# Letting background steps in between projection matmuls half as often, in bursts of up to twice the size

## The chip, the cores and the metric

The kernel runs on one core of one Trainium2 chip. The metric is the device time of one execution in microseconds (us), the median of several runs. PE is the matmul engine (TensorE), DVE is VectorE, ACT is ScalarE, POOL is GpSimd, and SP is the engine whose queue issues the transfers from HBM.

## What is computed

Two layers over 256 latent tokens and 256 context tokens of width 1024. Each layer is a token mixer and then an expert-choice mixture of 16 experts (MoE). The second layer needs the context only as keys, so its mixer works on 256 columns where the first works on 512. The reference, cut to the mixer:

```python
dq, dk, dv, hy, sq, sk, sv, gt = split_in(h @ p['w_in'])
q = apply_rope(dq.reshape((B, L) + qk_shape), cos, sin)
y_diff = diff_post(diff_latent(q, concat(k, kc), concat(v, vc), lam), ...)
y_hy = hyena(hy, p)                                   # short conv, long conv by a DFT
y_swa = swa_latent(s_q, s_k, s_v, s_kc, s_vc, sink)   # windowed attention with a sink
gs = jnp.split(sigmoid(gt), 3, axis=-1)
merged = sum(gs[b] * (ys[b] @ p['w_branch'][b]) for b in range(3))
y = merged @ p['w_out']
```

## The kernel before, in words

The program has no loop at run time. Python code writes out one fixed order of instructions for every engine, and a planner in it (`Model`, `Background`) decides that order while the program is being built: it keeps a guessed clock for each engine and guesses when each tile will be ready. On the chip every engine then works through its own list in that order and waits on semaphores where an operand is late.

A mixer is a list of 116 blocks (`mixer`). A block makes 128 output columns of one projection: its weights are loaded by SP (tile `wraw`), split by ACT, DVE and POOL into a high and a low part (`wh`, `wl`), and multiplied on PE in 24 matmuls into one PSUM bank, 8 of `wh` with `hhi`, 8 of `wh` with `hlo`, then 8 of `wl` with `hhi` (`yb` and `mg` take the place of `hhi` and `hlo` in later blocks). Blocks 0 to 52 of the mixer feed the attention and Hyena tasks, the later ones are gates, `w_branch` products, eight blocks for the windowed attention, and last, blocks 108 to 115, `w_out`.

Everything else of the mixer is background: tasks written as Python generators (`diff_gen`, `swa_gen`, `hyena_gen`, `filter`, `mod_run`, `mod_vec`). A task issues one **step** (some instructions on one or more engines) and then yields the tiles that its next step needs. A typical step issues a pair of score matmuls (`kp`, `kl` with `qp`), or the four transposes of a probability tile (a matmul of `cst` with an `arena` tile), or the product with the values (`arena` with `svt`), or only the ACT and DVE work between these.

Steps come into PE's list in four ways:

- `pump` (L367), called between the matmuls of a block and once after it: it takes steps whose tiles the planner thinks ready, while a credit lasts, while ACT and DVE are not too far behind, and at most `BURST` steps that used PE.
- `until` (L383), ahead of a block's matmul whose operand is late: it fills the gap.
- `slot` (L392), when the work behind a block (its evacuation, `b.evac`) needs a buffer of the arena and none is free: it forces the step that can run first, ready or not, until one is free.
- `drain` (L399): block 92 of the second mixer begins the third branch, which needs the windowed attention's results, so all of its remaining steps are forced there in one piece.

The calls between a block's matmuls stand at the end of the loop over `i` from 0 to 15, where `k` is `i % 8`; for `i` below 8 a pass issues two matmuls, from 8 on one:

```python
if i < KT or k % 2 and k < KT - 1:
    self.bg.pump()
```

The MoE's weights (tile `mw`) are first asked for late in the mixer, after certain blocks (`PREF`, L46, and `fill` at L1053): in the first mixer after blocks 108 to 111, in the second after blocks 87, 93, 108, 111 and 112. The rest is asked for as the MoE frees buffers.

Of the kernel before, what the change touches and what calls it, by code (L numbers as in the profile page):

```python
# [21 lines left out]
KT = 8  # L22
# [4 lines left out]
WCUT = (4, 4)  # L27
WIDTH = (4, 3)
BACKLOG = (1500.0, 750.0)
BURST = (6, 3)  # L30
SWA = 8
SWA_STEP = 2
RATE = (0.75, 0.6)
# [253 lines left out]
class Background:  # L287
# [79 lines left out]
    def pump(self, rate=None):  # L367
        self.credit = min(self.credit + (self.now - self.mark) * (rate or self.rate()), CREDIT[self.layer])
        n = 0
        while n < BURST[self.layer]:  # L370
            self.start()
# [37 lines left out]
class Kernel:  # L409
# [588 lines left out]
    def run_blocks(self, bl, ahead=2, first=3):  # L998
        nl = ns = first
        later = []  # L1000
        for j, b in enumerate(bl):
            self.bg.due, end = [], self.bg.now
            for c in bl[j:]:
                if c.drains:
                    self.bg.due.append((c.drains, end))
                end += 24 * (4.0 + 0.41 * c.n)
            while ns < min(max(j + ahead, first + (j > 0)), len(bl)):
                self.split_block(bl[ns], later if j else None)
                ns += 1
            while nl < len(bl) and (nl <= ns or (nl - ns < 3 and self.model.dead("a4", BUFS["a4"]) > SPARE[self.bg.layer])):  # L1010
                self.load_block(bl[nl])
                nl += 1
            if self.bg.layer and len(bl) - 1 - j == MODR:
                self.bg.add("mod", lambda task: self.mod_vec([(1, v) for v in range(3, 6)]))
            if j < first:
                while later:
                    later.pop(0)()
                if j == 0:
                    for c in bl[:first]:
                        if c.pre:  # L1020
                            c.pre()
                    hi, lo = b.hl()
                    ps = [self.bank([128, c.n], "d" if i < 2 else "b") for i, c in enumerate(bl[:first])]
                    for k in range(KT):
                        self.bg.until([hi[:, k], lo[:, k]])
                        for c, p in zip(bl, ps):
                            self.mm3(p, (c.wh[:, k], c.wl[:, k]), (hi[:, k, 0:c.n], lo[:, k, 0:c.n]), k == 0, k == KT - 1)
                b.wh = b.wl = None
                b.evac(ps[j])
                continue  # L1030
            if b.pre:
                b.pre()
            hi, lo = b.hl()[:2]
            p = self.bank([128, b.n], "d")
            for i in range(2 * KT):
                k = i % KT
                if i < KT:
                    self.bg.until([b.wh[:, k], hi[:, k], lo[:, k]])
                    self.mm(p, b.wh[:, k], hi[:, k, 0:b.n], i == 0, False)
                    self.mm(p, b.wh[:, k], lo[:, k, 0:b.n], False, False)  # L1040
                else:
                    self.bg.until([b.wl[:, k]])
                    self.mm(p, b.wl[:, k], hi[:, k, 0:b.n], False, k == KT - 1)
                if i >= LATER[self.bg.layer] and later:
                    later.pop(0)()
                if i > LATER[self.bg.layer] and nl < len(bl) and nl - ns < 3 and self.model.dead("a4", BUFS["a4"]) > SPARE[self.bg.layer]:
                    self.load_block(bl[nl])
                    nl += 1
                if i < KT or k % 2 and k < KT - 1:
                    self.bg.pump()  # L1050
            b.wh = b.wl = None
            if len(bl) - 1 - j in PREF[self.bg.layer]:
                self.fill(PREF[self.bg.layer][len(bl) - 1 - j])  # L1053
            b.evac(p)
            self.bg.pump()
# [1008 lines left out]
```

## Time and profile before

| | |
|---|---|
| median of 3 runs | 2575.46 us (2573.92 to 2581.18) |
| the profiled execution | 2579.04 us |
| its span, first to last instruction | 2577.3 us |
| PE busy | 2240.2 us, 87% of the span |
| DVE, ACT, POOL busy | 52%, 34%, 31% |
| granted PE clock, mean | 0.945 |
| first mixer, first projection matmul to the MoE | about 42 to 985 us |
| first MoE | about 985 to 1507 us |
| second mixer | about 1507 to 2102 us |
| second MoE and the end | about 2102 to 2577 us |

The profile is of one execution, taken by the hardware profiler. An engine's share is an average over four stages that have different limits, so it is read stage by stage. "Idle before" an instruction is the time its engine stood still just ahead of it, put down to what ended that wait. L458 is the helper that issues matmuls, L469 the one that issues transposes, and L261 the one through which all other engines' instructions go, so groups are told apart by their tiles.

### The profile page before, as it was taken

How to read it: one execution, taken by the hardware profiler on the slowest of the kernel's cores; microseconds unless marked ns; L12 is line 12 of the kernel's file. 1: busy time of each engine (PE TensorE's matmuls, PEld its weight loads, DVE VectorE, ACT ScalarE, POOL GpSimd, SP SyncE). 2: the span in 40 equal slices, each digit the busy share in tenths (PEclk: the TensorE clock that was granted, in tenths of full speed). 3: DMA queues.
4: the chain of work that ended last, by engine and by line, in shares of the span. 5: the costliest groups of instructions: out<-in, count | busy, mean ns of one | idle time of the engine just before them, and what ended most of it. 6: DMA issues, size and time to landing. Idle time of an engine off the chain costs nothing.

```text
span 2577.3 us, 38619 instructions
## 1 busy us (share of the span) xinstructions
PE 2240.2 (87%) x14970; PEld 1542.7 (60%) x14970; DVE 1347.2 (52%) x2907; ACT 882.1 (34%) x1933; POOL 794.8 (31%) x775
## 2 busy tenths in 40 slices
PE   6999998989999998989998899899888987656565
PEld 4777776767768775333333378878787864323223
DVE  4778778888672324223333178887887541101011
ACT  4445444555552332101111055556435441000001
POOL 2653433642334541000111055665544430000000
PEclk8999999999999999999999999999989989878787
DMA  9434233221213368899999963333665589999997
GB/s 304 123 122 126 89 109 106 58 66 50 66 58 91 95 252 316 331 428 417 398 400 399 398 185 97 104 95 84 177 190 164 130 317 423 422 424 423 424 423 278
DMA packets 327135, 590.32 MB, mean 229 GB/s; under 512 B 46076, under 2 KB 278184, under 8 KB 299304
## 3 DMA queue, kind: packets, MB, share of 16 engines
q1 hardware_dynamic: 326952, 587.85, 62.2%
q8 instruction: 119, 1.95, 0.3%
q14 instruction: 64, 0.52, 0.1%
HBM read 584.66 MB, written 3.15 MB: 228 GB/s over the span
## 4 chain that ended last, share of the span: by engine, by line
PE 47%; DMA 20%; DVE 20%; issue 4%; ACT 4%; POOL 3%; SPq 1%; DVEq 0%; POOLq 0%; ACTq 0%
PE p L458 44%; DMA mw<-in_moe_w_dram 19%; DVE arena L261 6%; DVE t L261 5%; PE p L469 3%; DVE wl L261 2%; DVE qp L261 2%; ACT arena L261 1%; DMA wm<-in_w_mod_dram 1%; POOL wl L261 1%; SPq L261 1%; POOL arena L261 1%; DVE ma L261 1%; DVE yc L261 1%; ACT wh L261 1%
## 5 line engine op out<-in xcount | busy, mean ns | idle before, releaser
L458 PE MATMUL p<-mw,xg 128*32 128x256 f32 (+1 forms) x3072 | 411.0, 508 | 115.3 <-DMA mw<-in_moe_w_dram 114.4
L458 PE MATMUL p<-hhi,wh 128*128 128x512 f32 (+1 forms) x1344 | 471.4, 363 | 10.1 <-DVE arena L261 7.7
L458 PE MATMUL p<-hlo,wh 128*128 128x512 f32 (+1 forms) x1344 | 458.9, 354 | 1.6 <-POOL hlo L261 0.8
L261 POOL TENSOR_TENSOR wl<-wraw,wh 128x512 fp32r<-128x512 f32 x232 | 342.5, 1478 | 374.8 <-ACT wh L261 251.8
L458 PEld LDWEIGHTS p<-mw,xg 128*32 128x32 f32 (+1 forms) x3072 | 133.7, 129 | 317.1 <-issue 200.0
L458 PE MATMUL p<-hhi,wl 128*128 128x512 f32 (+1 forms) x1344 | 312.9, 361 | 4.5 <-DVE wl L261 4.4
L458 PEld LDWEIGHTS p<-hhi,wh 128*128 128x128 f32 x1344 | 259.4, 193 | 48.5 <-issue 13.3
L458 PEld LDWEIGHTS p<-hlo,wh 128*128 128x128 f32 x1344 | 259.6, 193 | 31.4 <-POOL hlo L261 1.7
L458 PE MATMUL p<-mw,aT 128*32 128x256 f32 (+3 forms) x1760 | 200.4, 475 | 62.5 <-DMA mw<-in_moe_w_dram 58.2
L261 DVE TENSOR_TENSOR wl<-wraw,wh 128x512 fp32r<-128x512 f32 x231 | 217.0, 940 | 57.4 <-ACT wh L261 47.0
L261 ACT ACTIVATE wh<-wraw 128x1024 fp32r<-128x1024 f32 x232 | 241.4, 1053 | 9.0 <-DMA wraw<-in_w_in_dram 6.8
L458 PEld LDWEIGHTS p<-hhi,wl 128*128 128x128 f32 x1344 | 222.0, 194 | 37.0 <-DVE wl L261 5.2
L261 ACT ACTIVATE arena<-p 128x512 f32<-128x512 f32 (+1 forms) x212 | 106.4, 507 | 354.5 <-PE p L458 296.7
L458 PEld LDWEIGHTS p<-mw,aT 128*32 128x32 f32 (+1 forms) x1760 | 79.5, 134 | 172.3 <-issue 109.0
L261 DVE COPY yS<-p 32x512 f32<-32x512 f32 (+1 forms) x60 | 33.4, 556 | 272.9 <-ACT yS L261 272.9
L261 POOL TENSOR_TENSOR sq<-sq,sq 128x512 f32<-128x512 f32 (+1 forms) x6 | 6.3, 1055 | 505.6 <-ACT sq L261 498.8
L458 PE MATMUL p<-yb,wh 128*128 128x512 f32 (+1 forms) x768 | 153.6, 343 | 7.5 <-POOL yb L261 6.8
L261 ACT ACTIVATE arena<-p,t 128x512 f32<-128x512 f32 (+1 forms) x192 | 116.5, 613 | 84.7 <-DVE t L261 82.5
L458 PEld LDWEIGHTS p<-yb,wh 128*128 128x128 f32 x768 | 118.5, 190 | 26.8 <-POOL yb L261 11.6
L261 ACT ACTIVATE s<-p 128x512 f32<-128x512 f32 (+1 forms) x32 | 15.7, 491 | 337.1 <-PE p L458 336.9
L261 ACT ACTIVATE yS<-p 32x256 f32<-32x256 f32 (+2 forms) x84 | 35.3, 420 | 266.2 <-PE p L458 247.1
L469 PE MATMUL p<-cst,arena 128*128 128x128 f32 x608 | 101.0, 290 | 28.8 <-DVE arena L261 27.8
(243 smaller groups left out, 3451.4 us busy)
## 6 DMA issues: line engine op xcount, KB each, us to landing
mw<-in_moe_w_dram SPq DMA_DIRECT2D x171, 2048.0 KB
wraw<-in_w_in_dram SPq DMA_DIRECT2D x152, 512.0 KB
wm<-in_w_mod_dram SPq DMA_DIRECT2D x72, 512.0 KB
mw<-in_moe_w_dram SPq DMA_DIRECT2D x46, 512.0 KB
mw<-in_moe_w_dram SPq DMA_DIRECT2D x17, 1024.0 KB
wraw<-in_w_branch_dram SPq DMA_DIRECT2D x32, 512.0 KB
wm<-in_w_mod_dram SPq DMA_DIRECT2D x5, 2048.0 KB
wraw<-in_w_in_dram SPq DMA_DIRECT2D x32, 256.0 KB
```

The costliest lines, as they stand in the source:

```text
L261: return f(*args, **kw)
L458: self.nc.tensor.matmul(out, lhsT=lhsT, rhs=rhs, start=start, stop=stop, skip_group_check=tiles > 1)
L469: self.nc.tensor.transpose(out, in_, self.ident[:n, :n])
```

## The change

```diff
-BURST = (6, 3)
+BURST = (12, 6)
...
-                if i < KT or k % 2 and k < KT - 1:
+                if k % 2 and i < KT or k == 3 and i > KT:
                     self.bg.pump()
```

The two numbers of `BURST` are for the first and the second layer. Before, `pump` is called behind `i` = 0 to 7 and 9, 11 and 13, which is 11 times in a block; with the change behind `i` = 1, 3, 5, 7 and 11, which is 5 times. The call behind the evacuation of a block stays. The `BURST` bound also holds for the calls inside the MoE.

No instruction is added or taken away; they come in another order. Three places show it, all on PE. In the names, `p` is a PSUM bank, `wh` and `wl` are a block's weights, `hhi` and `hlo` the projection's input, `cst` with `arena` a transpose, `kp` or `kl` with `qp` scores, `arena` with `svt` a product with the values.

The second mixer, inside block 69, before, from the middle of its `wh` matmuls on:

```order
L458 MATMUL p_15403<-hlo_11520,wh_15342 128x256
L469 MATMUL p_15415<-cst_68,arena_11588 128x128 x4
L458 MATMUL p_15403<-hhi_11519,wh_15342 128x256
L458 MATMUL p_15403<-hlo_11520,wh_15342 128x256
L469 MATMUL p_15427<-cst_68,arena_11588 128x128 x4
L458 MATMUL p_15432<-kp_14684,qp_15258 128x512
L458 MATMUL p_15432<-kl_14685,qp_15258 128x512
```

The same block with the change, its last rows and the first of what stands between it and block 70:

```order
L458 MATMUL p_15285<-hlo_11520,wh_15230 128x256
L458 MATMUL p_15285<-hhi_11519,wl_15231 128x256 x8
L469 MATMUL p_15315<-cst_68,arena_11588 128x128 x4
L469 MATMUL p_15327<-cst_68,arena_11589 128x128 x4
L469 MATMUL p_15335<-cst_68,arena_11589 128x128 x4
L458 MATMUL p_15344<-arena_11588 128x128 x4
L458 MATMUL p_15351<-kp_14525,qp_15325 128x512
L458 MATMUL p_15351<-kl_14526,qp_15325 128x512
```

Before, two insertions stand between the matmuls of block 69 and none behind it. With the change the block runs without a break, and behind it stand 34 background matmuls in one piece, which the evacuation's wish for an arena buffer forces out.

The second mixer, between blocks 91 and 92 (the drain), its beginning before:

```order
L458 MATMUL p_16639<-yb_15784,wl_16568 128x256 x8
L458 MATMUL p_16679<-kp_16293,qp_16513 128x512
L458 MATMUL p_16679<-kl_16294,qp_16513 128x512
L458 LDWEIGHTS identb_407
L458 MATMUL p_16679<-mask_406,identb_407 128x128
L458 MATMUL p_16680<-kp_16293,qp_16513 128x512
L458 MATMUL p_16680<-kl_16294,qp_16513 128x512
L458 LDWEIGHTS identb_407
L458 MATMUL p_16680<-mask_406,identb_407 128x128
L469 MATMUL p_16696<-cst_68,arena_11589 128x128 x4
L469 MATMUL p_16702<-cst_68,arena_11589 128x128 x4
L469 MATMUL p_16715<-cst_68,arena_11588 128x128 x4
```

The same place with the change:

```order
L458 MATMUL p_16535<-yb_15704,wl_16491 128x256 x8
L469 MATMUL p_16583<-cst_68,arena_11588 128x128 x4
L469 MATMUL p_16591<-cst_68,arena_11588 128x128 x4
L469 MATMUL p_16603<-cst_68,arena_11588 128x128 x4
L469 MATMUL p_16609<-cst_68,arena_11588 128x128 x4
L458 MATMUL p_16614<-arena_11589,svt_14207 64x128
L458 MATMUL p_16614<-arena_11588,svt_14207 64x128
```

Two more attention tasks are left for the drain: it holds 164 matmuls before and 208 with the change, and from the tile `p_16696` on the two lists hold the same steps.

## Rows read from the trace of the kernel before

**Rows 1.** Busy time by stretch: from:to, us; then busy us of each engine, PEclk, DMA share, GB/s
```profile
62.00:985.00 923.00, 877.57 (x4762) 684.51 (x4762) 615.08 (x1332) 425.64 (x955) 401.44 (x396) 0.99 0.34 104
985.00:1507.00 522.00, 475.03 (x2531) 197.21 (x2533) 170.18 (x421) 78.55 (x179) 47.47 (x73) 0.97 0.96 387
1523.00:1982.00 459.00, 419.17 (x2863) 375.23 (x2863) 386.75 (x700) 236.18 (x458) 265.83 (x227) 0.96 0.46 135
1986.00:2025.00 39.00, 30.09 (x230) 23.08 (x229) 29.98 (x84) 22.31 (x61) 5.00 (x10) 0.82 0.07 21
2025.00:2102.00 77.00, 76.12 (x601) 71.11 (x600) 31.75 (x58) 36.91 (x81) 46.69 (x39) 1.00 0.91 284
2102.00:2577.00 475.00, 301.70 (x3630) 148.02 (x3628) 71.12 (x209) 42.65 (x120) 3.26 (x5) 0.82 0.96 397
```

**Rows 2.** Waits of PE, 62 to 985 us: waited for, us in total, times, longest us
```profile
PE p L469 <- DVE arena L261: 10.2, 12, 3.0
PE p L458 <- DVE qp L261: 6.6, 9, 2.0
```

**Rows 3.** Waits of PE, 1523 to 2102 us
```profile
PE p L469 <- DVE arena L261: 17.6, 16, 2.8
PE p L458 <- DVE arena L261: 8.2, 5, 3.3
PE p L458 <- DVE wl L261: 4.4, 4, 2.9
```

**Rows 4.** Waits of PE, 2102 to 2577 us
```profile
PE p L458 <- DMA mw<-in_moe_w_dram: 149.1, 72, 5.8
```

**Rows 5.** PE in order of time, second mixer, the drain: start us, us, instruction [idle before]
```profile
1986.69 0.23 PE L458 MATMUL p<-mask,identb 128*128 128x128 bf16 x1
1988.08 1.06 PE L469 MATMUL p<-cst,arena 128*128 128x128 f32 x8 [1.17 <-DVE arena L261]
1991.01 1.39 PE L469 MATMUL p<-cst,arena 128*128 128x128 f32 x8 [1.86 <-DVE arena L261]
...
2003.25 1.06 PE L469 MATMUL p<-cst,arena 128*128 128x128 f32 x8 [0.98 <-DVE arena L261]
...
2019.41 3.44 PE L469 MATMUL p<-cst,arena 128*128 128x128 f32 x16 [2.06 <-DVE arena L261]
...
2024.68 0.39 PE L458 MATMUL p<-hhi,wh 128*128 128x256 f32 x1
```

**Rows 6.** PE in order of time: steps let in between matmuls without a wait
```profile
608.31 1.09 PE L458 MATMUL p<-arena,svt 128*64 128x128 f32 x16
609.34 0.66 PE L469 MATMUL p<-cst,arena 128*128 128x128 f32 x4
609.75 0.71 PE L458 MATMUL p<-hhi,wl 128*128 128x512 f32 x2
...
1978.93 0.40 PE L458 MATMUL p<-kp,qp 128*128 128x512 f32 x1
...
1981.22 0.36 PE L458 MATMUL p<-hhi,wh 128*128 128x256 f32 x1
```

**Rows 7.** SP's transfers in order of time, around the drain
```profile
1986.59 2.57 SPq L261 DMA_DIRECT2D wraw<-in_w_branch_dram  x4
2026.95 0.35 SPq L261 DMA_DIRECT2D mw<-in_moe_w_dram  x1
...
2078.71 57.19 SPq L261 DMA_DIRECT2D mw<-in_moe_w_dram  x28
```

**Rows 8.** PE in order of time, first mixer: an insertion, then matmuls without one
```profile
600.36 0.38 PE L469 MATMUL p<-cst,arena 128*128 128x128 f32 x2
600.50 0.48 PE L458 MATMUL p<-hhi,wh 128*128 128x512 f32 x1
600.81 0.39 PE L458 MATMUL p<-hlo,wh 128*128 128x512 f32 x1
...
601.49 0.40 PE L458 MATMUL p<-hlo,wh 128*128 128x512 f32 x1
601.72 0.39 PE L458 MATMUL p<-hhi,wh 128*128 128x512 f32 x1
```

## The prediction, made before the changed kernel ran

> **What bounds the kernel now.** I read busy time by stretch first, then PE's waits in each mixer, then PE and SP in order of time around the drain. In both mixers PE is the bound: it is busy 877.57 of 923.00 us in the first and 419.17 of 459.00 us in the second up to its drain, while DMA runs at a third to a half of its time [rows 1]. What PE does not work there is 45.4 and 39.8 us, in short waits, mostly for DVE: 12 of them last 10.2 us and 16 last 17.6 us, so 0.85 and 1.1 us each [rows 2, 3]. The drain is a stretch of its own: in 39.00 us PE is busy for 30.09, at a granted clock of 0.82, so a part of it at the lower of its two levels, 1.2 GHz, after waits of 1 to 2 us [rows 1, 5]. The second MoE waits 149.1 us for its weights [rows 4], with DMA at 0.96 of its time [rows 1]. Does a longer mixer then cost anything? Yes: through the drain SP issues nothing of `mw` (none between 1986.59 and 2026.95), and 28 of its loads start only at 2078.71 [rows 7], behind blocks that PE reaches only after the drain. The first MoE's weights are asked for behind blocks 108 to 111. So PE time won or lost in either mixer moves all that follows by as much.
>
> **The change, part by part.** The work is the same: between the first and the last projection matmul the order holds 1534 background matmuls in the first mixer and 785 in the second, both before and after, and the same transfers. Only places move. There are 113 blocks behind the first three, so `pump` is called 113 x 12 = 1356 times in a mixer before and 113 x 6 = 678 times with the change. Yet the order shows 259 insertions in the first mixer and 99 in the second before, and 207 and 80 with the change: most calls found nothing to take. So insertions fall by 71, a fifth, not by half.
>
> *Fewer insertions.* Behind a transpose the next projection matmul takes 0.31 us to its successor's start (600.50 to 600.81), in an unbroken run 0.23 (601.49 to 601.72) [rows 8]. 71 x 0.08 = 5.7 us won. Not every kind of step costs that much, so it is 3 to 6; I take 5.5.
>
> *The drain.* Before, from the end of its first score pair at 1986.92 to 2024.68 it takes 37.8 us [rows 5]. It holds 16 groups of transposes, 8 products with the values and 5 more score pairs. Where such steps are let in without a wait, a product takes 1.03 us (608.31 to 609.34), a group of transposes 0.41 (609.34 to 609.75), and two score pairs 2.29 (1978.93 to 1981.22) [rows 6], so this work would take 8 x 1.03 + 16 x 0.41 + 5 x 1.15 = 20.5 us. The drain loses 17.3 us on it, through waits and the lower clock: 0.60 us for each of the 29 groups, 0.11 us for each of 158 matmuls. With the change 44 more matmuls stand there: 44 x 0.11 = 4.8 us. Their 2 tasks could fit into waits that are there anyway (0). Or they make one more whole round like the one from 2003.25 to 2019.41, 16.2 us [rows 5] with some 9 us of work in it (3 products, 3 pairs, 6 transpose groups), a loss of 7. I take 5. What is issued less between the blocks before it is PE time given back, and is left out of both sides.
>
> A rule of the Trainium skill speaks against this change: the page "Perfetto Trace Analysis", section "Optimization Strategy", says that performance may be improved by interleaving stretches with different busiest engines. Taken by the words of the change, half the interleaving would be lost: half of 1534 + 785 matmuls at the drain's 0.11 us would be some 127 us by that reading, an estimate. The drain agrees with the rule's direction; that so much cover is lost is not borne out, since the order leaves all but some 160 of these matmuls between or behind blocks as they were.
>
> *Runs forced by a full arena.* Background that progresses later holds its buffers longer. Behind blocks 39 and 45 of the first mixer and 41 and 69 of the second, where the evacuation asks for a buffer, the new order has runs of 20, 30, 28 and 34 matmuls in one piece between a block's last `wl` matmul and the next block's first. Before, the only such run stands behind block 73 of the second mixer, 20 long, with data mostly there. The new runs have 24 groups in all (a Hyena product, then its transposes, then `mod` or attention steps), that depend on each other through ACT and DVE as in the drain. At the drain's 0.60 us a group that is 14 us. If every group waited as an average wait in the first mixer, 24 x 0.85 = 20 us; if the steps were ready, 0. I take 12, near the drain, as a few of the groups are of tasks that do not wait for each other.
>
> *Steps let in later.* A call now comes every second pair of matmuls, so a step is let in on average half a pair-time later: one matmul of 512 columns, 0.23 us [rows 8], in the first mixer, half of that in the second. A wait of 0.85 us shrinks by at most 0.23, or 27% of 45.4 = 12 us; 0.12 of 1.1 us is 11% of 39.8 = 4 us. So up to 16 us are won. Against it: more steps at once put a longer line into DVE, which ends most waits, and in that line stand the split of the weights (4.4 us of waits) and the evacuation of the blocks (within 8.2 us) [rows 3]. The same 16 us bounds it from above. I take 3 us won.
>
> *The higher bound of a burst* costs nothing by itself: the mean insertion grows only from 5.9 to 7.4 matmuls and from 7.9 to 9.8. In the first mixer SP's loads of `wm` and of the filter stand elsewhere among the `wraw` loads; the cover is a DMA share of 0.34 [rows 1]. If that went, a late `wraw` would show as a wait for `wh`, and PE has none worth a row now.
>
> Sum: 5 + 12 - 5.5 - 3 = 8.5 us. On the profiled execution's own 2579.0 us that is 2587.5. The median shown is 2575.5, 3.6 us below it, so the forecast is 2584 us, 0.33% slower. About 0.3% (8 us) is what a measurement of this kernel can tell from no change, so the forecast lies at that edge.
>
> **The rivals.** *Faster, by waits that vanish.* If the waits in the mixers are mostly steps let in a little too early, the full 16 us come back, and the forced runs cost nothing because what they hold is ready: 5 - 5.5 - 16 = -16.5, 2559 us; with half of the runs' price -10.5, 2565 us. For it: nearly all waits are for DVE and short. Against it: 0.23 us is little beside 0.85. It decides once the forced runs cost under 6 us in all.
>
> *It does little.* Insertions fall by only a fifth. If forced runs cost 6 instead of 12 us the sum is 2.5 us: 2578 us, nothing to be told. For it: before, the first mixer has runs of 24 and 26 matmuls that were let in ready, with no loss of the drain's kind.
>
> *Slower, by a queue on DVE.* The bursts delay evacuations and weight splits. Then the two rows of 8.2 and 4.4 us [rows 3] double, the waits do not shrink, and the forced runs cost 20 us: 5 + 20 - 5.5 + 12.6 = 32 us, 2608 us. For it: three waits of a projection's first matmul for a bank that DVE frees are among the longest of the second mixer (up to 3.3 us). Against it: `pump` still stops while DVE is behind.
>
> **How the numbers follow.** The forecast's own case (forced runs at 8 to 16 us, waits about as before) has 0.42, the queue on DVE 0.10, little effect 0.28, faster 0.20. Its own range is 2578 to 2592. The forecast case reaches a little under the edge and the case of little effect a little over it, which cancel: slower by over 0.3% 0.52, within 0.28, faster 0.20. The ends with all bounds together are 5.5 + 16 = 21.5 us won (2554) and 7 + 20 + 16 - 3 = 40 us lost (2616). Cutting a tenth from each side gives 2562 to 2604.
>
> **What would show it.** Right: PE's drain lasts 47 to 55 us instead of 39 with its clock still near 0.8; behind blocks 39, 45, 41 and 69 stand runs with waits on DVE and ACT of 2 to 4 us in sum each; PE's total work is unchanged; both MoEs last as long as before, moved. Wrong: idle time in the mixers outside these runs falls by over 10 us, or grows by it; PE waits for `wh` or `wraw`; or the second MoE starts later but ends no later.

## The result, and the profile after

The changed kernel takes 2600.48 us (median of 4 runs, 2596.33 to 2603.86); the kernel before, on the same chip, 2577.01 us (2573.92 to 2581.18). The ratio is 1.0088 with a 95% interval of 1.0072 to 1.0104, so the change costs 0.0088 x 2577.0 = 22.7 us, between 18.6 and 26.8. The forecast was 2584 us, 8.5 us more than before: the sign and the main places were right, the size was too small by a factor of 2.7. The measured time lies above the forecast case's own range (2578 to 2592 us), and near the slow end of the whole range (2562 to 2604).

The busy time by stretch of the changed kernel, in the columns of [rows 1]:

```profile
62.00:998.00 936.00, 886.37 (x4767) 690.84 (x4766) 623.54 (x1332) 425.81 (x956) 398.04 (x397) 0.99 0.34 103
998.00:1517.00 519.00, 475.95 (x2527) 197.72 (x2529) 169.29 (x418) 77.62 (x177) 47.52 (x73) 0.97 0.96 389
1534.00:1994.00 460.00, 414.98 (x2814) 371.12 (x2813) 381.29 (x677) 230.37 (x441) 259.17 (x224) 0.96 0.47 134
1997.00:2049.00 52.00, 36.52 (x292) 27.84 (x293) 42.22 (x115) 28.92 (x80) 7.11 (x14) 0.87 0.04 11
...
2125.00:2598.00 473.00, 298.28 (x3632) 144.40 (x3630) 71.19 (x209) 42.68 (x121) 3.52 (x5) 0.82 0.96 398
```

The first mixer is 13 us longer, the drain lasts 52 us instead of 39 with a granted clock of 0.87, and the two MoEs are 3 and 2 us shorter. To compare like with like, two stretches are cut at the same matmuls in every kernel: "first mixer" is the start of the first matmul of block 3 to that of block 108, "second mixer" that of block 3 to that of block 92, the drain included. The kernel before, in the same columns:

```profile
62.00:932.82 870.82, 825.93 (x4517) 645.37 (x4517) 598.13 (x1302) 401.16 (x878) 383.35 (x381) 0.99 0.32 94
1523.18:2024.68 501.50, 452.79 (x3121) 401.80 (x3121) 420.24 (x789) 261.01 (x525) 271.62 (x237) 0.95 0.43 125
1982.74:2024.68 41.94, 33.03 (x255) 25.84 (x253) 32.93 (x90) 25.02 (x68) 5.97 (x10) 0.84 0.09 26
```

The changed kernel:

```profile
62.34:945.46 883.12, 834.02 (x4518) 651.11 (x4517) 606.25 (x1302) 400.99 (x878) 379.74 (x381) 0.98 0.31 93
1534.34:2048.42 514.08, 453.26 (x3120) 400.83 (x3121) 423.09 (x789) 261.82 (x525) 266.29 (x238) 0.95 0.43 122
1993.61:2048.42 54.81, 38.98 (x314) 30.10 (x313) 42.10 (x113) 31.97 (x86) 7.46 (x14) 0.88 0.07 20
```

In each, the third row is block 91 and the drain behind it. The two profiled spans differ by 2597.6 - 2577.3 = 20.3 us, and it adds up: first mixer +12.3, the stretch to the second mixer (945.46 to 1534.34, before 932.82 to 1523.18) -1.5, second mixer up to block 91 -0.3, block 91 with the drain +12.9, all behind it -3.4, the start +0.3. PE's work in numbers of matmuls is the same. In the first mixer PE idles 49.1 us instead of 44.9 and is busy 8.1 us longer; in the second it idles 60.8 instead of 48.7. Ahead of block 91 in the second mixer, PE's busy time falls by 5.5 us and its idle time rises by 5.2.

**The forced runs.** Behind block 45 of the first mixer, PE in order of time, in the columns of [rows 5]:

```profile
451.83 1.18 PE L458 MATMUL p<-hhi,wl 128*128 128x512 f32 x4
452.94 0.64 PE L458 MATMUL p<-wm,sc 128*32 128x256 f32 x8
455.06 0.68 PE L458 MATMUL p<-arena,arena 128*128 128x128 f32 x4 [1.48 <-DVE arena L261]
455.50 1.67 PE L458 MATMUL p<-yf,ft 128*128 128x256 f32 x12
458.24 0.66 PE L469 MATMUL p<-cst,yt 128*128 128x128 f32 x4 [1.07 <-ACT yt L261]
458.82 0.64 PE L458 MATMUL p<-wm,sc 128*32 128x256 f32 x8
463.67 1.11 PE L469 MATMUL p<-cst,yd 128*128 128x128 f32 x4 [4.21 <-DVE yd L261]
464.44 0.78 PE L458 MATMUL p<-hhi,wh 128*128 128x512 f32 x1
```

DVE at the same place:

```profile
457.18 2.37 DVE L261 TENSOR_TENSOR arena<-arena,K 128x512 f32<-128x512 f32 x2
459.48 1.72 DVE L261 TENSOR_SCALAR t<-t 128x4 f32<-128x4 f32 x4
461.16 0.16 DVE L261 TENSOR_TENSOR t<-t 128x4 f32<-128x4 f32 x1
461.36 0.16 DVE L261 TENSOR_TENSOR t<-t,t 128x4 f32<-128x4 f32 x1
...
462.73 0.16 DVE L261 SCALAR_TENSOR_TENSOR t<-t,t 128x4 f32<-128x4 f32 x1
462.93 0.69 DVE L261 TENSOR_TENSOR yd<-yd,t 128x512 f32<-128x512 f32 x1
```

PE stands still three times, 6.76 us in all, and the last time for 4.21 us: just as long as DVE needs for a chain of 13 small instructions (a reciprocal root in `t`, 4 values in each partition) and the scaling of `yd`, 459.48 to 463.62. Ahead of that chain in DVE's list stands 2.37 us of another task's product. The run takes 11.5 us (452.94 to 464.44) for work of 4.2 (2 x 0.64, 0.44, 1.67 and two groups of transposes at 0.41 [rows 6]).

The other three runs, each ending with the next block's first matmul. Behind block 39 of the first mixer, 41 and 69 of the second (the row at 1883.51 is still block 69's own):

```profile
389.87 0.51 PE L458 MATMUL p<-yf,ft 128*128 128x256 f32 x3
391.38 0.38 PE L458 MATMUL p<-yf,ft 128*128 128x256 f32 x1 [0.99 <-ACT yf L261]
392.72 1.22 PE L458 MATMUL p<-yf,ft 128*128 128x256 f32 x8 [0.96 <-POOL yf L261]
395.54 1.06 PE L469 MATMUL p<-cst,yd 128*128 128x128 f32 x4 [1.60 <-DVE yd L261]
...
397.11 0.78 PE L458 MATMUL p<-hhi,wh 128*128 128x512 f32 x1
...
1728.45 0.47 PE L458 MATMUL p<-kp,qp 128*128 128x512 f32 x1 [0.39 <-DVE qp L261]
...
1729.66 0.50 PE L458 MATMUL p<-kp,qp 128*128 128x512 f32 x1 [0.50 <-DVE qp L261]
...
1731.16 0.47 PE L458 MATMUL p<-kp,qp 128*128 128x512 f32 x1 [0.30 <-DVE arena L261]
...
1731.81 1.67 PE L458 MATMUL p<-yf,dfth 128*128 128x256 f32 x12
1734.29 0.66 PE L469 MATMUL p<-cst,yt 128*128 128x128 f32 x4 [0.81 <-ACT yt L261]
1738.76 1.11 PE L469 MATMUL p<-cst,arena 128*128 128x128 f32 x4 [3.81 <-DVE arena L261]
1739.53 0.56 PE L458 MATMUL p<-hhi,wh 128*128 128x256 f32 x1
...
1883.51 1.86 PE L458 MATMUL p<-hhi,wl 128*128 128x256 f32 x8 [1.76 <-DVE wl L261]
1885.17 2.47 PE L469 MATMUL p<-cst,arena 128*128 128x128 f32 x12
...
1891.58 0.39 PE L458 MATMUL p<-hhi,wh 128*128 128x256 f32 x1
```

They take 7.2, 11.5 and 6.4 us. The first holds 12 matmuls and 8 transposes, 1.67 + 0.82 = 2.5 us of work. The second runs from 1728.06 to 1739.53: ahead of the same kind of work stand two forced score steps, 8 matmuls of 512 columns (1.8 us at 0.23 each [rows 8]), with waits of 0.39, 0.50 and 0.30 us, so it has 4.3 us of work and waits of 5.8 us in all. The third has no wait in it. So in place the four lose 4.7 + 7.3 + 7.1 + 0 = 19.1 us. The third is not free either: its 12 transposes take 2.47 us, where three groups would take 1.23 [rows 6], but the wait of 1.76 us that precedes them is one of block 69's own matmuls, so this is not added here. Short windows of PE, three behind the runs, one ahead of the run behind block 45, and one over the run behind block 69:

```profile
397.00:403.00 6.00, 6.00 (x32) 4.35 (x31) 4.75 (x8) 2.00 (x3) 3.92 (x3) 0.83 0.01 1
464.00:470.00 6.00, 6.00 (x23) 4.88 (x21) 4.75 (x8) 2.64 (x4) 3.35 (x3) 0.73 0.01 4
1739.00:1745.00 6.00, 6.00 (x31) 5.91 (x31) 3.98 (x8) 2.51 (x5) 3.18 (x2) 0.60 0.05 15
446.00:452.00 6.00, 5.29 (x34) 4.46 (x33) 4.51 (x10) 2.74 (x10) 4.05 (x3) 1.00 0.39 126
1885.00:1892.00 7.00, 6.87 (x55) 5.44 (x55) 6.84 (x14) 2.42 (x6) 0.00 (x0) 0.84 0.44 126
```

In the first three PE is busy for all of the 6 us, at granted clocks of 0.83, 0.73 and 0.60, so 34, 54 and 80% of the time at the lower level, 1.2 GHz. In the 6 us from 446 us, ahead of the run, the clock was 1.00. By an estimate from these clocks the three windows cost another 6 x (0.17 + 0.27 + 0.40) = 5.0 us. But the kernel before has such stretches too, at other places. Added up over windows of 4 us, PE's busy time times what its clock lacked of 1.00 is 7.6 us in the first mixer before and 10.6 with the change, 21.9 and 19.5 in the second: 3.0 us more and 2.4 us less. So over both mixers the lower clock costs about the same in both kernels.

**The drain**, PE in order of time (from 1996.65, where block 91 ends, to the first matmul of block 92):

```profile
1995.53 1.12 PE L458 MATMUL p<-yb,wl 128*128 128x256 f32 x8
2002.76 3.65 PE L469 MATMUL p<-cst,arena 128*128 128x128 f32 x16 [6.11 <-DVE arena L261]
...
2048.42 0.39 PE L458 MATMUL p<-hhi,wh 128*128 128x256 f32 x1
```

Before, the drain began with score matmuls [rows 5] that needed nothing new; now it begins with transposes, and PE waits 6.11 us for the first of them.

**Other waits of PE** in the changed kernel, for the second mixer (1534 to 2123 us) as in [rows 3]:

```profile
PE p L469 <- DVE arena L261: 19.7, 11, 6.1
PE p L458 <- DVE arena L261: 7.7, 4, 5.2
PE p L458 <- DVE wl L261: 4.9, 4, 1.8
```

Over the whole run:

```profile
PE p L469 <- DVE yd L261: 20.0, 12, 4.9
```

The same row before:

```profile
PE p L469 <- DVE yd L261: 8.1, 6, 4.0
```

It is the row that grew most, by 11.9 us. The forced runs hold 5.8 us of it (1.60 and 4.21), and a wait of 4.91 us stands inside block 38 of the second mixer.

### The profile page after: what moved, and what is told of

The parts are those of the page before. It is cut to its first block, busy times and chain, and to the rows that moved or that the text cites. A ratio compares the mean times of both kernels' runs of the same rounds, so it can differ in the third digit from the quotient of the medians.

```text
span 2597.6 us, 38636 instructions
## 1 busy us (share of the span) xinstructions
PE 2245.8 (86%) x14970; PEld 1545.3 (59%) x14970; DVE 1356.8 (52%) x2907; ACT 882.2 (34%) x1933; POOL 785.3 (30%) x775
## 4 chain that ended last, share of the span: by engine, by line
PE 48%; DMA 20%; DVE 18%; ACT 5%; issue 4%; POOL 3%; SPq 1%; DVEq 0%; POOLq 0%; ACTq 0%
PE p L458 45%; DMA mw<-in_moe_w_dram 18%; DVE t L261 5%; DVE arena L261 5%; PE p L469 3%; DVE wl L261 2%; ACT arena L261 2%; DVE qp L261 1%; DMA wraw<-in_w_in_dram 1%; DMA wm<-in_w_mod_dram 1%; ACT wh L261 1%; POOL wl L261 1%; SPq L261 1%; DVE ma L261 1%; DVE yc L261 1%
## 5 line engine op out<-in xcount | busy, mean ns | idle before, releaser
L261 POOL TENSOR_TENSOR wl<-wraw,wh 128x512 fp32r<-128x512 f32 x232 | 332.6, 1435 | 437.1 <-ACT wh L261 357.4
L458 PE MATMUL p<-hhi,wl 128*128 128x512 f32 (+1 forms) x1344 | 307.1, 360 | 6.6 <-DVE wl L261 4.9
L458 PE MATMUL p<-mw,aT 128*32 128x256 f32 (+3 forms) x1760 | 195.2, 460 | 57.5 <-DMA mw<-in_moe_w_dram 53.8
```

What stands on the lines that cost most here:

```text
L261: return f(*args, **kw)
L458: self.nc.tensor.matmul(out, lhsT=lhsT, rhs=rhs, start=start, stop=stop, skip_group_check=tiles > 1)
```

## The experiments

The theory: halving the calls makes the background late, and it is paid for where a late step is forced, by a full arena (behind a block) or by the drain, whether its data are there or not. Rivals: that fewer calls cost by themselves; that longer bursts hold up DVE; that the steps left to the drain are the whole loss. The following table has all twelve runs. A forced group is a step that used PE and was issued by `slot` or `drain`, counted in the order of each kernel; "arena + drain" are those of the second mixer, and one group of each drain count stands only behind block 115. The lengths are those of the stretches above, from each kernel's own profile.

| kernel | calls in a block | `BURST` | ratio to before, 95% interval | first mixer, us (forced) | second mixer, us (arena + drain) | block 91 and drain, us |
|---|---|---|---|---|---|---|
| before | 11 | 6, 3 | 1 | 870.8 (0) | 501.5 (4 + 31) | 41.9 |
| changed | 5 | 12, 6 | 1.0088 [1.0072, 1.0104] | 883.1 (11) | 514.1 (15 + 39) | 54.8 |
| burst_alone | 11 | 12, 6 | 1.0026 [1.0012, 1.0040] | 871.2 (0) | 507.6 (6 + 16) | 24.0 |
| calls_alone | 5 | 6, 3 | 1.0182 [1.0163, 1.0200] | 883.3 (11) | 532.3 (27 + 40) | 57.7 |
| calls_second_only | 11, 5 | 12, 6 | 1.0044 [1.0028, 1.0059] | 868.8 (0) | 512.9 (15 + 39) | 54.0 |
| half_calls_deeper_second | 5 | 12, 6 | 1.0031 [1.0019, 1.0044] | 883.2 (11) | 494.6 (0 + 4) | 10.7 |
| half_calls_deeper_both | 5 | 12, 6 | 1.0007 [0.9994, 1.0020] | 876.6 (0) | 495.5 (0 + 4) | 10.7 |
| before_deeper_both | 11 | 6, 3 | 1.0023 [1.0006, 1.0039] | 872.3 (0) | 502.3 (5 + 1) | 2.9 |
| seven_calls | 7 | 12, 6 | 1.0065 [1.0043, 1.0087] | 873.1 (0) | 511.7 (30 + 8) | 15.9 |
| fifteen_calls | 15 | 6, 3 | 1.0017 [1.0005, 1.0029] | 878.6 (0) | 496.3 (1 + 12) | 25.1 |
| second_5_calls_free | 11, 5 | 6, 6 | 0.9997 [0.9985, 1.0009] | 871.0 (0) | 494.5 (0 + 4) | 10.7 |
| second_7_calls_free | 11, 7 | 6, 6 | 0.9998 [0.9985, 1.0012] | 871.1 (0) | 502.6 (0 + 3) | 7.9 |
| second_11_calls_free | 11 | 6, 6 | 0.9974 [0.9962, 0.9986] | 870.3 (0) | 492.7 (0 + 5) | 13.2 |
| second_15_calls_free | 11, 15 | 6, 6 | 0.9961 [0.9947, 0.9976] | 870.4 (0) | 496.0 (0 + 4) | 7.5 |

Two numbers of calls are for the first and the second mixer. `BACKLOG` is 1500, 750 (ns, one number for each mixer) unless a diff says otherwise: `pump` takes nothing while the work that is queued on ACT and DVE exceeds it by the planner's clock, so a larger number lets more steps in early. All diffs are against the kernel before; where a diff has only `+` lines, the lines that they replace are left out. The same order repeats well: the changed kernel's first mixer stands in three kernels and took 883.1, 883.3 and 883.2 us; that of before stands in seven and took 868.8 to 871.2. The changed kernel's second mixer stands in two (514.1 and 512.9), that of half_calls_deeper_second in three (494.6, 495.5 and 494.5). What follows the second mixer varies more, 547.6 to 552.6 us in the fourteen profiles, partly in other orders.

### The two parts alone

```diff
-BURST = (6, 3)
+BURST = (12, 6)
```

> Only the bound of a burst is raised (12 and 6), the calls stay 11 in a block. PE's order is the same as before up to the second mixer; there the drain holds 82 matmuls instead of 164, and the arena forces a few groups more. Theory (what costs is steps that are forced, in the drain or for an arena buffer): the drain gets 7 to 10 us shorter than its 39 us, forced groups take some of it back, so 2570 to 2580 us, same as before. Rival (larger bursts put a longer line into DVE, and this is what made the change slower): second mixer longer by 8 to 13 us, 2585 to 2590 us, with more idle outside forced runs.

Measured: 2581.33 us, ratio 1.0026. The first mixer is unchanged. In the second the drain shrinks as 82 of its 164 matmuls are let in earlier, yet the mixer is 6.1 us longer:

```profile
1520.83:2028.40 507.57, 449.71 (x3120) 394.59 (x3120) 427.62 (x789) 262.00 (x524) 267.22 (x237) 0.97 0.42 124
```

PE's idle time is 57.9 us there, 9.2 more than before, though fewer groups are forced. So the number of forced groups is not the whole of it. The median lies 1 us above the theory's range and 4 below the rival's, the mixer's 6.1 us below the rival's 8 to 13: a longer line on DVE is not excluded as the cause of these 6 us.

```diff
-                if i < KT or k % 2 and k < KT - 1:
+                if k % 2 and i < KT or k == 3 and i > KT:
```

> Calls halved, burst bound left at 6 and 3. The first mixer's order is that of the change; in the second the order holds 27 groups forced by the arena and 40 in the drain, 67 against 54 with the change. Theory (about 0.6 us lost for each forced group): 8 us longer than with the change, about 2608 us. Rival (the bound of the burst is what costs, the calls do not): no longer than the kernel before in the second mixer, about 2588 us.

Measured: 2621.52 us, ratio 1.0182, 13 us more than the 2608 expected. The halved calls alone cost some 47 us (0.0182 x 2573.4), twice the whole change:

```profile
1535.83:2068.17 532.34, 463.08 (x3120) 408.14 (x3120) 411.31 (x789) 260.55 (x524) 266.93 (x237) 0.93 0.40 118
```

The first mixer is the changed kernel's; the second is 18.2 us longer still, at a clock of 0.93. So the two parts do not add up (0.26% and 1.82%, together 0.88%): with half the calls the higher bound of a burst gives back some 24 us. The forced groups of the second mixer fall with it from 67 to 54; that the late steps catch up by it is argued from that.

### One mixer at a time

```diff
+BURST = (12, 6)
+                if (k % 2 and i < KT or k == 3 and i > KT) if self.bg.layer else (i < KT or k % 2 and k < KT - 1):
```

> Calls halved in the second mixer alone, burst bound raised in both: the first mixer's order is that of before, the second's that of the change. Theory (each mixer loses by its own forced runs): half of the loss stays, the first mixer is back at about 943 us, the second as long as with the change, 2585 to 2592 us. Rival (the loss comes from one cause shared by both, so a mixer alone shows little or all of it): 2577 or 2600 us.

Measured: 2586.27 us, ratio 1.0044: the first mixer is before's (868.8), the second the changed kernel's (512.9). Each mixer holds about half of the loss.

```diff
+BACKLOG = (1500.0, 1500.0)
+BURST = (12, 6)
+                if k % 2 and i < KT or k == 3 and i > KT:
```

> The change as it is, but in the second mixer a call goes on until ACT or DVE are planned to be 1500 ns behind PE instead of 750. The calls stay halved, yet in the second mixer the order now has no run forced by the arena and a drain of 24 matmuls instead of 208. Theory (forced runs and drain are the loss): the second mixer falls by its loss of 12 us and by most of what the drain lost before already (17 us), 2572 to 2582 us. Rival (steps let in in bursts wait for a longer line on DVE): the second mixer stays as long as with the change or gets longer, 2598 us or more, with idle moved from the drain to between the blocks.

Measured: 2584.29 us, ratio 1.0031. The first mixer keeps its forced runs and its 883.2 us. In the second only 4 forced groups are left of 54, and it is 19.5 us shorter than the changed kernel's, and 6.9 shorter than before's. The whole kernel is 2 us above the 2572 to 2582 expected.

```diff
+BACKLOG = (3000.0, 1500.0)
+BURST = (12, 6)
+                if k % 2 and i < KT or k == 3 and i > KT:
```

> The change with both bounds on how far ACT and DVE may be behind doubled (3000 and 1500 ns). The order has no run forced by the arena in either mixer and a drain of 24 matmuls; calls stay halved. Theory: as the run before it, and the first mixer falls by its 12 us too, 2560 to 2570 us, faster than the kernel before. Rival (longer line on DVE): idle in short waits grows in both mixers by over 15 us each, 2600 us or more.

Measured: 2577.32 us, ratio 1.0007 with an interval that holds 1, though 2560 to 2570 us were expected. So with half the calls, and nothing forced in the first mixer, the kernel is back at the time of before:

```profile
62.55:939.17 876.62, 826.20 (x4518) 646.19 (x4517) 606.66 (x1302) 400.25 (x878) 384.92 (x381) 0.99 0.31 94
1527.33:2022.85 495.52, 448.88 (x3121) 396.54 (x3121) 418.85 (x789) 261.39 (x525) 269.50 (x238) 0.96 0.43 127
```

PE is busy 826.20 us in the first mixer, as before, not 834.02. The clock explains 3.3 of these 7.8 us (7.3 us where the changed kernel has 10.6, by the sum over windows of 4 us); the rest stays open. But this is no proof that half the calls cost nothing. The first mixer stays 5.8 us above before's, as idle time (50.4 us), and the total is level only because the second is 6.0 us shorter than before's, for which the deeper line is there as well. Of the first mixer's waits one row grew most, 62 to 940 us:

```profile
PE p L469 <- DVE arena L261: 20.6, 22, 3.0
```

In the changed kernel that row is 9.4 us, 15 times, and before it is 10.2 [rows 2]. With twice the line allowed on DVE, PE waits at transposes for data that DVE has not made yet. A single wait of 4.6 us for `wl` is new too, and other rows are smaller.

### Is the deeper line the gain?

```diff
+BACKLOG = (3000.0, 1500.0)
```

> The kernel before, all 11 calls, with both bounds on how far ACT and DVE may be behind doubled. The first mixer has no forced run with or without this, so it shows what a longer line on DVE costs: theory 5 to 8 us more there (PE's transposes wait for DVE's copies, as with the halved calls and the same bounds); rival: nothing, and then the halved calls themselves cost what the first mixer kept. In the second mixer the drain goes (1 group of 31 is left): 488 to 496 us up to block 92 instead of 502. In all 2570 to 2580 us.

Measured: 2578.48 us, ratio 1.0023. The deeper line alone gains nothing with before's calls: the second mixer takes 502.3 us, where 488 to 496 were expected, although almost nothing is left to the drain (2.9 us with block 91). What the drain had lost is lost between the blocks instead. In the first mixer it costs only 1.5 us, where 5 to 8 were expected, so the deeper line alone does not explain the 5.8 us above. Whether they belong to half the calls by themselves, as the rival says, or to both together is not shown: no run has half the calls there with neither the forced runs nor the deeper line.

### Other numbers of calls

```diff
+BURST = (12, 6)
+                if k % 2 and i < KT or i > KT and k % 2 and k < KT - 1:
```

> Seven calls in a block instead of 5 (behind passes 1, 3, 5, 7, 9, 11, 13), burst bounds 12 and 6. In the first mixer no run is forced by the arena any more (224 insertions), the bounds on ACT's and DVE's line as before. In the second 30 groups are forced by the arena and 8 in the drain, 38 in all (35 before, 54 with the change). Theory (forced groups are the loss): first mixer, from block 3 to block 108, at 868 to 873 us as before (883 with the change); second up to block 92 within 5 us of the 502 before; 2575 to 2582 us. Rival (fewer calls cost by themselves): first mixer at 877 us or more.

Measured: 2591.41 us, ratio 1.0065, where 2575 to 2582 us were expected. Two calls more in a block take the forced runs out of the first mixer, and with them 10.0 of the 12.3 us. The second mixer stays bad at 511.7 us, where about 502 were expected: only 8 forced groups are in its drain, but 30 stand behind blocks, and the mixer is 10 us longer than before's with 35 in all.

```diff
+                if i < 2 * KT - 1:
```

> More calls than before: behind 15 of the 16 passes of a block, everything else as before. The drain falls from 31 groups to 12 and the arena forces 1 instead of 4. Theory (forced groups): 8 to 13 us shorter in the second mixer, the first about as before (no run is forced there), 2564 to 2570 us, faster than the kernel before. Rival (each insertion costs, and steps let in earlier wait longer for DVE): 2577 us or more.

Measured: 2580.08 us, ratio 1.0017: slower, not the 2564 to 2570 us expected, and as the rival has it. The second mixer is 5.2 us shorter, with 13 forced groups for 35. The first is 7.8 us longer, with nothing forced in either. There PE waits 11.1 us for `yd` instead of 3.2, but in all it idles only 3.4 us longer and is busy 4.4 us longer; the cause stays open.

### With nothing forced in the second mixer

These four leave the first mixer as it was, and in the second allow a burst of 6 and a line deep enough that the drain holds 3 to 5 groups and the arena forces none. The line is not the same in all: 1500 ns with 5 and 7 calls, 1000 ns with 11 and 15.

```diff
+BACKLOG = (1500.0, 1500.0)
+BURST = (6, 6)
+                if (k % 2 and i < KT or k == 3 and i > KT) if self.bg.layer else (i < KT or k % 2 and k < KT - 1):
```

> First mixer's order that of the kernel before. Second mixer: 5 calls in a block, bursts up to 6, ACT and DVE up to 1500 ns behind: no group forced by the arena, 4 in the drain. Theory (only forced groups cost, not the number of calls): 495 us from block 3 to block 92 as measured with the same settings, 7 us less than before, 2566 to 2572 us. Rival (halved calls cost by themselves in the second mixer too): slower than the runs of this set with 7, 11 and 15 calls by over 4 us.

```diff
+BACKLOG = (1500.0, 1500.0)
+BURST = (6, 6)
+                if (k % 2 and k < KT - 1 or i == KT - 1) if self.bg.layer else (i < KT or k % 2 and k < KT - 1):
```

> As the run with 5 calls, but 7 calls in a block of the second mixer: no group forced by the arena, 3 in the drain. Theory: within 3 us of the run with 5 calls, 492 to 498 us from block 3 to block 92, 2566 to 2572 us. Rival (halved calls cost): faster than that run by 2 to 4 us.

```diff
+BACKLOG = (1500.0, 1000.0)
+BURST = (6, 6)
```

> All 11 calls in both mixers; in the second bursts up to 6 and ACT and DVE up to 1000 ns behind: no group forced by the arena, 5 in the drain. Theory: 492 to 498 us from block 3 to block 92, 2566 to 2572 us, so that 5, 7, 11 and 15 calls come out alike. Rival (halved calls cost): faster than with 5 calls by over 4 us.

```diff
+BACKLOG = (1500.0, 1000.0)
+BURST = (6, 6)
+                if i < 2 * KT - 1 if self.bg.layer else (i < KT or k % 2 and k < KT - 1):
```

> 15 calls in a block of the second mixer, bursts up to 6, ACT and DVE up to 1000 ns behind: no group forced by the arena, 4 in the drain; the first mixer as before. Theory: 492 to 498 us from block 3 to block 92, 2566 to 2572 us. Rival (insertions cost): slower than with 5 calls by 3 us or more.

Measured: 2572.23, 2573.11, 2568.25 and 2563.60 us, beside 2573.07 before. The second mixer takes 494.5, 502.6, 492.7 and 496.0 us with 5, 7, 11 and 15 calls. These lengths show no trend with the number of calls: with 5 the mixer is 1.8 us longer than with 11. The 7-call order fell outside the 492 to 498 us expected, with 53.4 us of idle time against 44.9 to 46.4 in the other three. But the medians of the whole kernel do fall from 5 and 7 calls to 11 and 15, and the profiles of the 7-call and the 15-call kernel are of the slowest of their executions (2582.26 and 2567.80 us). Between 5 and 11 calls the medians differ by 4.0 us, at the edge of the "over 4 us" that the rival of costly halved calls asked for; 15 calls are 8.6 us faster than 5, and 7 calls no faster. So with next to nothing forced, halving the calls costs the second mixer little; that it costs the kernel nothing is not shown. Both mixers together say the same: against second_11_calls_free (0.9974), half_calls_deeper_both (1.0007) is slower by 0.33%, 8.5 us, of which the profiles have 6.3 us in the first mixer, where its line is deeper, and 2.8 us in the second.

second_15_calls_free beats both kernels: 0.9961 [0.9947, 0.9976], some 10 us less than before.

```profile
1520.07:2016.09 496.02, 451.09 (x3121) 398.98 (x3121) 422.47 (x789) 261.51 (x524) 266.19 (x236) 0.96 0.43 127
```

Of the 11.3 us between the two profiled spans, 5.5 are in the second mixer; 3.1 are ahead of it and 2.7 behind, where the order is nearly the same, and by these single profiles they can't be told from scatter.

Over all fourteen kernels the second mixer's length goes with its forced groups: a straight line through the table has 494.3 us and 0.43 us a group, with points 4.7 us off it in the mean (root of the mean square), a correlation of 0.90. That is somewhat under the 0.60 us a group that the prediction read from the drain, and it leaves several us that depend on the order in a way that no count here explains.

## Why the prediction was right in sign and too small

**Runs forced by a full arena: right place, mis-sized.** This is the step that failed. The prediction put the drain's 0.60 us on each of 24 groups and took 12 us. The four runs lose 19.1 us in place, near the upper bound of 20, and with the 5.0 in the windows behind them 24 us. Two things were left out. A forced run is no average of its groups: the one behind block 45 waits out a chain of small DVE instructions ahead of `yd` (4.21 us), and one whose steps are ready (block 69) waits for nothing. And the price goes on after the run, since PE comes out of it at the lower clock; the prediction read that in the drain's 0.82 but did not carry it to the blocks behind the runs. That is true of these places; over both mixers the lower clock costs hardly more than before (30.1 us by the sums above, where it was 29.5). The prediction's own sign, waits of 2 to 4 us in sum behind each of the four blocks, holds for one of them: they are 3.6, 6.8, 5.8 and 0 us. That these runs cause at least half of the first mixer's loss is shown: kernels with them take 883 us, and without them, by 11, 7 or 15 calls or a deeper line, 869 to 879.

**The drain: right, a little small.** The stretch from the end of block 91's matmuls (1996.65 to 2048.42) is 51.8 us, within the 47 to 55 forecast, at a clock of 0.87. Block 91 with the drain grew by 12.9 us. Of that, 4 transpose groups, 2 products and 2 pairs are work moved in, 4 x 0.41 + 2 x 1.03 + 2 x 1.15 = 6.0 us by [rows 6], so the loss is 6.9 us, where 5 was taken and 7 was the upper end. But the blocks ahead of it, which lost that work, became hardly shorter (459.6 us from block 3 to 91 before, 459.3 now): the 7.1 us of the forced run behind block 41 are more than that.

**Fewer insertions: not seen.** The 5.5 us do not show. PE's busy time in the first mixer is 825.9 us with 259 insertions (before), 826.2 with 219 (half_calls_deeper_both), 828.8 with 224 (seven_calls), 827.4 with 250 (before_deeper_both) and 830.3 with 245 (fifteen_calls): no trend. The 0.08 us at one insertion [rows 8] was no price that holds for all.

**Steps let in later: a gain, twice what was taken.** Outside the two forced runs the first mixer idles 49.1 - 6.8 - 3.6 = 38.7 us instead of 44.9, so 6 us were won there. In the second mixer, ahead of block 91 and outside the run behind block 41 (5.8 us), it is 45.0 - 5.8 = 39.2 instead of 39.8. That is 6.8 us in all; taken were 3, of up to 16. Against it came a wait that was not foreseen: inside block 38 of the second mixer PE waits 4.91 us for `yd`, at a step that a call let in as ready. It is in the 39.2.

**The sum** by measured terms: 24.1 + 6.9 - 6.8 = 24.2 us; the stretches outside the mixers give back 1.5 + 3.4 - 0.3 = 4.6, which the prediction held at nothing. That makes 19.6 of the 20.3 us between the profiles. Part of this agreement is luck: mixer by mixer the terms give 8.4 us in the first, which grew by 12.3, and 15.8 in the second, which grew by 12.6. The forecast's 8.5 us had likewise two terms that were off in opposite ways, beside the runs: the 5.5 us of fewer insertions, which did not come, and some 4 us more from steps let in later.

**The rivals.** "Faster" and "little" needed forced runs at 6 us or less; they cost 19 to 24. "A queue on DVE" would double the waits of projection matmuls for `arena` and `wl`: they are 7.7 and 4.9 us, where they were 8.2 and 4.4 [rows 3], so that mechanism did not come, though the measured time is nearer to its 2608 us than to the forecast's 2584. A line on DVE does cost in half_calls_deeper_both, at transposes, not at the evacuations.

The rule that the prediction quoted from the Trainium skill ("Perfetto Trace Analysis", "Optimization Strategy"), that interleaving stretches with different busiest engines may improve performance, agrees in direction: half the calls alone lose 47 us. But 15 calls for 11 in both mixers lose too (1.0017), so more of it is no gain by itself. The same section says that a gap which repeats can mean that there is too little room in SBUF or PSUM for the next tile. The forced runs resemble that case: three of the four have waits of 3.6 to 6.8 us where the arena is full. The direct test, an arena with one more slab, was not run. So a full arena as the cause is shown only by ways of emptying it earlier, which also change the order elsewhere.

**Still open:** why the first mixer is 7.8 us longer with 15 calls and 5.8 longer with half the calls and a deeper line, whether half the calls cost some of that by themselves, what makes up the 3.9 us of the first mixer that no term covers, and why orders that force nothing differ by up to 10 us in the second mixer (492.7 to 502.6).

## What to carry to other kernels

When a fixed order is thinned out, look first for where the delayed work must be done whatever happens (a full buffer, a due date): most of the loss sat there, in a few places, and not in the hundreds of places that were thinned. Price such a place by its own chain on the other engines, not by an average of waits, and look at the clock behind it, but compare the lower clock's whole cost with that of before. A setting that looks bad may be bad only through a bound beside it: here half the calls cost 47 us with the old bounds, 23 with a longer burst, and 2 once a deeper line kept the arena from filling. Then give the old setting the same help: 11 calls with bounds that force nothing behind a block are 7 us faster than before, so half the calls still trail by 8.5.

## What was not expected of the hardware

A chain of DVE instructions on 4 values in each partition takes as long as real work: each lasts 0.16 us and the next starts 0.20 us after it (461.16, 461.36), four of another form 0.42 us each, so 13 of them with the scaling behind take 4.1 us, more than twice the 1.67 us of 12 matmuls of 256 columns. And behind the three forced runs with waits (3.6, 6.8 and 5.8 us of them, in runs of 7.2, 11.5 and 11.5 us) PE was busy without a break for 6 us at a granted clock of 0.83, 0.73 and 0.60, where the 6 us ahead of the second had 1.00.
